# The last two products of an encoder block by one level of Strassen's scheme, in its form with fifteen sums

## The chip, the cores and the metric

One core of a Trainium2 chip runs the whole block. The metric is device time in microseconds, and lower is better. TensorE multiplies, VectorE (DVE) and ScalarE (ACT) do the work on single elements, GpSimd (POOL) adds in SBUF, and SyncE (SP) issues most of the transfers.

## The reference

512 tokens of width 2048 pass through two branches (gated DeltaNet attention and a convolution module), which are mixed with two gates. The part that matters here is what follows:

```python
gate_a, gate_b = jnp.split(jax.nn.sigmoid(gate_logits + b_gate[i]), N_BRANCHES, axis=-1)
mixed = (gate_a * y_a + gate_b * y_b) @ w_out[i]
x = x + rmsnorm(mixed, g_post[i])

e = p[i] @ w_ple_proj[i]
x = x + rmsnorm(jax.nn.sigmoid(x @ w_ple_gate[i]) * e, g_ple[i])
```

`w_out` and `w_ple_gate` are 2048 x 2048, in float32. The second product needs the normalised result of the first, and so all of its columns.

## The kernel before

Every float32 operand is split into two parts in TensorE's faster float32 format: `hi` is a cast on ACT, `lo` the rest, subtracted on VectorE. A product is then three matmuls, hi by hi, hi by lo and lo by hi, of 128 x 128 by 128 x 512 each.

Most products run in `gemm_cm` (L163), with weights as the stationary operand: a bank named `g` collects 128 output columns for all 512 tokens. `w_br_b`, the branch's last product, is interleaved with the gates of `gate_b`. The evacuation `evac_yb` (L815) forms the mixed input, 16 tiles of 128 channels by 512 tokens (`mixed`, in the profile `gt`), and the generator `split_mixed` (L826) splits them into `mh` and `ml`. It is driven by `tick`, once in some matmuls.

Then follow the two products at issue, in `gemm_tm` (L864). Here the activations are the stationary operand: a bank named `f` holds 128 tokens by 512 output columns, and four banks, one per token tile, are summed over 16 steps of 128 channels. One step uses one half of a loaded `raw` tile, split 512 wide in `prep` (L113), up to three halves ahead. w_out runs in column blocks of 512; the last block runs for the low token tiles (0, 1) and then for the high ones (2, 3), so that its weights are loaded and split twice. `out_evac` (L904) forms squares for the norm and multiplies by `g_post`. The generator `post` (L921) adds the residual and transposes x1 on TensorE (`x1t`) and splits it, low tokens beside the products of the high ones. w_ple_gate follows in the same way. Its last block is split ahead and kept whole (`hold`), and runs token tile by token tile, each with its norm and its output. The power -0.5 for a norm is a small GpSimd instruction (L889).

Each engine works through its own list in order. The lists are written by a scheduler from the program's order and the free buffers of each pool, and semaphores hold an instruction back until what it needs is there.

Of the kernel before, what the change touches and what calls it, by code (L numbers as in the profile page):

```python
# [81 lines left out]
def _body(ctx, tc, A, out):  # L82
# [30 lines left out]
    def prep():  # L113
        if not prep_src:
            return
        src = prep_src.popleft()
        raw = ring.tile([P, 1024], F32, tag="raw", name="raw", bufs=3)
        nc.sync.dma_start(raw, src)
        for q in range(2):
            rq = raw[:, q * T:(q + 1) * T]  # L120
            hi = ring.tile([P, T], F32R, tag="hi", name="hi")
            nc.scalar.copy(hi, rq)  # L122
            lo = ring.tile([P, T], F32R, tag="lo", name="lo")
            nc.vector.tensor_tensor(lo, rq, hi.bitcast(F32), ALU.subtract)  # L124
            prepped.append((hi, lo))
# [689 lines left out]
    def evac_yb(i):  # L815
        def f(ps):
            gt = gate_b[i]
            nc.vector.tensor_tensor(gt, ps, gt, ALU.mult)  # L818
            m = mixed[i]
            nc.vector.tensor_tensor(m, m, gt, ALU.add)  # L820
            added[0] += 1
        return f

    added = [0]

    def split_mixed():  # L826
        for i in range(NK):
            while added[0] <= i:
                yield
            mh = hpool.tile([P, T], F32R, tag="h", name="mh")  # L830
            nc.scalar.copy(mh, mixed[i])
            ml = hpool.tile([P, T], F32R, tag="h", name="ml")
            nc.vector.tensor_tensor(ml, mixed[i], mh.bitcast(F32), ALU.subtract)
            mixT[i] = (mh, ml)
            yield

    gemm_cm(w_in_tile(GATE_TILE0 + 16), hT, evac_gate(gate_b, 0, 16))
    gemm_cm(w_in_tile(GATE_TILE0 + 17), hT, evac_gate(gate_b, 1, 17))
    jobs.append(finish)
    for i in range(NK):  # L840
        if i + 2 < NK:
            gemm_cm(w_in_tile(GATE_TILE0 + 18 + i), hT, evac_gate(gate_b, i + 2, 18 + i))
        else:
            jobs.append(lambda i=i: spawn(split_mixed(), 6, "mix") if i == NK - 2 else None)
# [10 lines left out]
    s3 = ctx.enter_context(tc.tile_pool(name="s3", bufs=40))  # L855
# [3 lines left out]
    LOW, HIGH, ALL = (0, 1), (2, 3), (0, 1, 2, 3)  # L859

    def queue_w(w, j):
        prep_src.extend(w[j, kp] for kp in range(8))

    def gemm_tm(lhs, evac, tts=ALL, side=None):  # L864
        ps = {tt: fps.tile([P, T], F32, tag="f", name="f") for tt in tts}
        for k in range(NK):
            wh, wl = next_piece()
            if side:
                side(k)
            for tt in tts:  # L870
                lh, ll = lhs(k, tt)
                mm(ps[tt], lh, wh, start=k == 0, stop=False)  # L872
# [24 lines left out]
    def mix_lhs(k, tt):
        return [t[:, tt * P:(tt + 1) * P] for t in mixT[k]]

    def x1_lhs(k, tt):  # L900
        b = (k % 2) * 256 + (tt % 2) * P
        return [t[:, b:b + P] for t in x1T[k // 2, tt // 2]]

    def out_evac(j, gp):  # L904
        def f(tt, ps):
            junk = slots.tile([P, T], F32, tag="s", name="fjunk")
            nc.scalar.activation(junk, ps, AF.Square, accum_out=ssm[:, tt, j:j + 1])
            mg = slots.tile([P, T], F32, tag="s", name="mg")
            nc.vector.tensor_tensor(mg, ps, gp, ALU.mult)
            x1[tt][j] = mg  # L910
        return f

    def load_x_again(tts):
        xr = {}
        for j in range(4):
            for tt in tts:
                xr[tt, j] = s3.tile([P, T], F32, tag="s3", name="xr")
# [3 lines left out]
    def post(tts, xr):  # L921
        rm = inv_rms(ssm[:, tts[0]:tts[0] + 2, :], f"m{tts[0]}")
        for j in range(4):
            for n, tt in enumerate(tts):
                nc.vector.scalar_tensor_tensor(x1[tt][j], x1[tt][j], rm[:, n:n + 1], xr[tt, j], ALU.mult, ALU.add)
            yield
            for k2 in (2 * j, 2 * j + 1):
                ps = fps.tile([P, T], F32, tag="f", name="x1t")
                for n in range(4):
                    k = 2 * k2 + n // 2  # L930
                    nc.tensor.transpose(ps[:, n * P:(n + 1) * P], x1[tts[n % 2]][j][:, (k % 4) * P:(k % 4 + 1) * P], ident)
# [3 lines left out]
                nc.vector.tensor_tensor(xl, ps, xh.bitcast(F32), ALU.subtract)
                x1T[k2, tts[0] // 2] = (xh, xl)
                yield

    def stepper(gen):
        def f(k):  # L940
            next(gen, None)
        return f

    for j in (0, 1, 2, 3, 3):
        queue_w(A["w_out"], j)
    for j in (0, 0, 1, 2):
        queue_w(A["w_ple_gate"], j)
# [8 lines left out]
    for _ in pgen:
        pass

    e_t = [[None] * 4 for _ in range(NTT)]

    def load_e(j):
        for tt in range(NTT):
            e_t[tt][j] = hpool.tile([P, T], F32, tag="h", name="e")
            nc.sync.dma_start(e_t[tt][j], pe_dram[j, tt])

    held = []
    hold_raw = {}

    def hold(k):
        if k % 2 == 0:  # L970
            hold_raw[0] = ring.tile([P, 1024], F32, tag="raw", name="raw", bufs=3)
            nc.sync.dma_start(hold_raw[0], A["w_ple_gate"][3, k // 2])
        rq = hold_raw[0][:, (k % 2) * T:(k % 2 + 1) * T]
        pool, th, tl_ = (hpool, "h", "h") if k < 8 else (s3, "s3", "s3") if k < 12 else (ring, "hi", "lo")
        hi = pool.tile([P, T], F32R, tag=th, name="hi")
        nc.scalar.copy(hi, rq)
        lo = pool.tile([P, T], F32R, tag=tl_, name="lo")
        nc.vector.tensor_tensor(lo, rq, hi.bitcast(F32), ALU.subtract)
        held.append((hi, lo))

    def ple_last(gp):
        def f(tt, ps):
            e = e_t[tt][3]
            sg = slots.tile([P, T], F32, tag="s", name="fsg")
            for h in range(2):
                c = slice(h * 256, h * 256 + 256)
                nc.scalar.activation(sg[:, c], ps[:, c], AF.Sigmoid)
                nc.vector.tensor_tensor(e[:, c], sg[:, c], e[:, c], ALU.mult)
                junk = slots.tile([P, T], F32, tag="s", name="fjunk")
                nc.scalar.activation(junk[:, c], e[:, c], AF.Square, accum_out=ssp[:, tt, 3 + h:4 + h])  # L990
            nc.vector.tensor_tensor(sg, e, gp, ALU.mult)
            e_t[tt][3] = sg
        return f

    def ple_evac(j, gp):
        def f(tt, ps):
            sg = slots.tile([P, T], F32, tag="s", name="fsg")
            nc.scalar.activation(sg, ps, AF.Sigmoid)
            s = e_t[tt][j]
            nc.vector.tensor_tensor(s, sg, s, ALU.mult)  # L1000
            junk = slots.tile([P, T], F32, tag="s", name="fjunk")
            nc.scalar.activation(junk, s, AF.Square, accum_out=ssp[:, tt, j:j + 1])
            nc.vector.tensor_tensor(s, s, gp, ALU.mult)
        return f

    gp = bcast_row(A["g_ple"], 0)
    load_e(0)
    pgen = post(HIGH, xr)
    gemm_tm(x1_lhs, ple_evac(0, gp), LOW, stepper(pgen))
    for _ in pgen:  # L1010
        pass
    gemm_tm(x1_lhs, ple_evac(0, gp), HIGH)
    load_e(1)
    gemm_tm(x1_lhs, ple_evac(1, bcast_row(A["g_ple"], 1)))
    load_e(2)
    load_e(3)
    gemm_tm(x1_lhs, ple_evac(2, bcast_row(A["g_ple"], 2)), ALL, lambda k: hold(k) if k < 12 else None)
    last = ple_last(bcast_row(A["g_ple"], 3))
    for k in range(12, NK):
        hold(k)  # L1020
    for tt in range(NTT):
        ps = fps.tile([P, T], F32, tag="f", name="f")
# [67 lines left out]
```

## Time and profile before

| | us |
|---|---|
| median of 3 runs | 2553.9 (2553.58 to 2555.51) |
| profiled execution | 2555.11 |
| its span | 2553.1 |
| last `g` matmul ends, evacuation starts | 2183.6 |
| first and last start of an `f` matmul | 2184.4, 2543.4 |
| TensorE busy over the span | 2521.1 (99%) |
| VectorE busy | 1597.5 (63%) |
| ScalarE busy | 1043.1 (41%) |
| GpSimd busy | 127.3 (5%) |

The span is that of one execution under the profiler, and its own time stands 2.0 us above it. A row of a timeline or of a group names the line, the engine, the operation and output<-inputs; in brackets stands the idle time before and what ended it. PE matmuls overlap, so their rate is read from the starts.

### The profile page before, as it was taken

What the parts mean: (1) busy time and instruction counts of PE and PEld (TensorE: products, weight loads), DVE (VectorE), ACT (ScalarE), POOL (GpSimd) and SP (SyncE); (2) the same over time, 40 slices, a digit from 0 to 9 for tenths busy, and PEclk for the clock granted to TensorE, in tenths of its full rate; (3) what the DMA queues carried; (4) which work ended last, traced back from release to release, by engine and by line L of the source; (5) the groups of instructions that cost most, each with busy time, mean ns of one, the idle gap of its engine ahead of it and who ended that gap; (6) DMA issues with size and microseconds to landing.
All of it is one profiled execution on the core that took longest, in us unless ns stands there. A gap on an engine that the chain in (4) does not pass through costs nothing.

```text
span 2553.1 us, 32961 instructions
## 1 busy us (share of the span) xinstructions
PE 2521.1 (99%) x12298; PEld 2051.1 (80%) x12298; DVE 1597.5 (63%) x3024; ACT 1043.1 (41%) x2083; POOL 127.3 (5%) x135
## 2 busy tenths in 40 slices
PE   8999999999999999999999999999999999999998
PEld 7878787787878777888888888888888888888886
DVE  6775767767576766886877778947423334336644
ACT  6655455455645555322222222235322223224542
POOL 0101010000101000000000000011000000000000
PEclk9999999999999999999999999999999999999999
DMA  7322222222222222323333333343323223436542
GB/s 255 128 81 69 83 79 75 79 83 87 63 91 71 75 75 83 107 95 108 101 102 103 105 98 107 97 160 99 99 92 98 94 96 100 165 103 204 181 152 70
DMA packets 82528, 268.99 MB, mean 105 GB/s; under 512 B 9152, under 2 KB 9408, under 8 KB 82368
## 3 DMA queue, kind: packets, MB, share of 16 engines
q1 hardware_dynamic: 81216, 264.79, 32.0%
q10 hardware_dynamic: 1152, 2.10, 0.3%
q8 instruction: 96, 1.57, 0.3%
q14 instruction: 64, 0.52, 0.1%
HBM read 252.17 MB, written 14.68 MB: 105 GB/s over the span
## 4 chain that ended last, share of the span: by engine, by line
PE 88%; DVE 7%; issue 2%; ACT 2%; DMA 0%; POOL 0%; SPq 0%; DVEq 0%; POOLq 0%; ACTq 0%
PE g L180 23%; PE g L178 23%; PE g L176 22%; PE f L872 4%; PE f L874 4%; PE f L873 4%; DVE prod L589 2%; DVE lo L124 2%; DVE VT L590 2%; PE psS L467 1%; PE psB L462 1%; DVE cv L404 1%; PE psA L456 1%; PE pg L557 1%; ACT VP L601 0%
## 5 line engine op out<-in xcount | busy, mean ns | idle before, releaser
L122 ACT CAST hi<-raw 128x512 fp32r<-128x512 f32 x860 | 530.9, 623 | 1164.2 <-PE g L178 945.9
L124 DVE TENSOR_TENSOR lo<-raw,hi 128x512 fp32r<-128x512 f32 x860 | 607.8, 710 | 621.5 <-ACT hi L122 600.8
L180 PE MATMUL g<-hh,lo 128*128 128x512 f32 x2320 | 917.4, 395 | 3.7 <-DVE lo L124 2.8
L176 PE MATMUL g<-hh,hi 128*128 128x512 f32 x2320 | 914.2, 394 | 4.0 <-DVE cv L404 2.5
L178 PE MATMUL g<-hl,hi 128*128 128x512 f32 x2320 | 917.0, 395 | 0.0
L180 PEld LDWEIGHTS g<-hh,lo 128*128 128x128 f32 x2320 | 436.3, 188 | 98.5 <-DVE lo L124 14.2
L176 PEld LDWEIGHTS g<-hh,hi 128*128 128x128 f32 x2320 | 436.2, 188 | 91.5 <-issue 5.5
L178 PEld LDWEIGHTS g<-hl,hi 128*128 128x128 f32 x2320 | 436.2, 188 | 86.5 <-issue 1.6
L671 DVE SCALAR_TENSOR_TENSOR uc<-sg,vec,uc 128x483 f32<-128x483 f32 (+15 forms) x480 | 351.7, 735 | 15.0 <-ACT uc L668 5.1
L404 DVE SCALAR_TENSOR_TENSOR cv<-g,vec,cv 128x511 f32<-128x511 f32 x144 | 107.6, 747 | 2.1
L872 PE MATMUL f<-hi,mh 128*128 128x512 f32 x256 | 100.3, 392 | 0.9 <-DVE gt L818 0.9
L180 PE MATMUL g<-uh,lo 128*128 128x512 f32 x256 | 100.9, 394 | 0.0
L176 PE MATMUL g<-oh,hi 128*128 128x512 f32 x256 | 100.9, 394 | 0.0
L178 PE MATMUL g<-ol,hi 128*128 128x512 f32 x256 | 100.9, 394 | 0.0
L180 PE MATMUL g<-oh,lo 128*128 128x512 f32 x256 | 100.9, 394 | 0.0
L176 PE MATMUL g<-uh,hi 128*128 128x512 f32 x256 | 100.9, 394 | 0.0
L178 PE MATMUL g<-ul,hi 128*128 128x512 f32 x256 | 100.9, 394 | 0.0
L874 PE MATMUL f<-hi,ml 128*128 128x512 f32 x256 | 99.8, 390 | 0.0
L873 PE MATMUL f<-lo,mh 128*128 128x512 f32 x256 | 99.7, 390 | 0.0
L589 DVE TENSOR_TENSOR prod<-UT,VT 128x2 f32<-128x2 f32 (+30 forms) x248 | 87.4, 352 | 7.2
L872 PE MATMUL f<-hi,xh 128*128 128x512 f32 x192 | 76.1, 396 | 0.0
L874 PE MATMUL f<-hi,xl 128*128 128x512 f32 x192 | 75.4, 393 | 0.0
(243 smaller groups left out, 2444.7 us busy)
## 6 DMA issues: line engine op xcount, KB each, us to landing
raw<-in_w_in SPq DMA_DIRECT2D x290, 512.0 KB, 3.4
raw<-in_w_out SPq DMA_DIRECT2D x40, 512.0 KB, 3.4
raw<-in_w_ple_gate SPq DMA_DIRECT2D x40, 512.0 KB, 3.7
raw<-in_w_br_a SPq DMA_DIRECT2D x32, 512.0 KB, 3.3
raw<-in_w_br_b SPq DMA_DIRECT2D x32, 512.0 KB, 3.3
x<-in_x SPq DMA_DIRECT2D x8, 512.0 KB, 9.2
pe_dram<-e_sb SPq DMA_DIRECT2D x16, 256.0 KB, 5.0
u_dram<-uc SPq DMA_DIRECT2D x16, 256.0 KB, 2.8
```

The lines of the kernel that those rows point to most:

```text
L122: nc.scalar.copy(hi, rq)
L124: nc.vector.tensor_tensor(lo, rq, hi.bitcast(F32), ALU.subtract)
L176: mm(ps, wh, rh, start=(k == 0), stop=False)
L178: mm(ps, wh, rl, start=False, stop=False)
L180: mm(ps, wl, rh, start=False, stop=(k == NK - 1))
L404: nc.vector.scalar_tensor_tensor(y[:, s:], ps[:, 0:T - s], vv(w0 + 3 - s), y[:, s:], ALU.mult, ALU.add)
L589: nc.vector.tensor_tensor(pv_, um, vm, ALU.mult)
L590: nc.vector.tensor_reduce(VT[:, j, i0:8], pv_, AX, ALU.add)
L671: nc.vector.scalar_tensor_tensor(y[:, s:], u[:, 0:T - s], vv(w0 + TAPS - 1 - s), y[:, s:], ALU.mult, ALU.add)
L872: mm(ps[tt], lh, wh, start=k == 0, stop=False)
L873: mm(ps[tt], lh, wl, start=False, stop=False)
L874: mm(ps[tt], ll, wh, start=False, stop=k == NK - 1)
```

## The change

Tokens, channels (K) and the columns of a half of the output (1024) are each cut into two. With A the activations and B the weights, seven products take the place of eight: `P1` = A11 by B11, `P2` = A12 by B21, and five of sums: `Q5`, `P6`, `P7`, `P3`, `Q4`. The names of the sums: S1 to S4 for activations (S1 = A21 - A22, S2 = S1 - A11, S3 = A11 - A21, S4 = A12 + S2), `t` (tile `tb`) for weights. A product has 48 matmuls for one half of the columns: four pieces of 256 channels (`q`), two token tiles (`t`), two steps of 128 and three parts.

```diff
+    def split_b():
+        for k2 in range(4):
+            s1 = Sf.pop(k2)
+            s3_ = s3.tile([P, T], F32, tag="s3", name="sf")
+            for n in range(2):
...
+                nc.gpsimd.tensor_tensor(s3_[:, c], mixed[kk][:, LO], mixed[kk][:, HI], ALU.subtract)
+                nc.gpsimd.tensor_tensor(s1[:, c], s1[:, c], mixed[kk][:, LO], ALU.subtract)
+            AW["S3"][k2] = sw_split(hpool, "h", s3_)
+            yield
+            AW["S2"][k2] = sw_split(hpool, "h", s1)
...
+    def load(w, jp, blk, q):
+        raw = s3.tile([P, 1024], F32, tag="rw", name="rw", bufs=5)
+        nc.sync.dma_start(raw, w[jp, blk, q])
+        return raw
+    def e_p1(w, jp, q):
+        b11 = load(w, jp, B11, q)
+        b12 = load(w, jp, B12, q)
+        t = tb[q] = s3.tile([P, 1024], F32, tag="t", name="t", bufs=4)
+        nc.gpsimd.tensor_tensor(t, b11, b12, ALU.add)
+        return [b11]
+    def e_a(w, jp, q):
+        return e_p1(w, jp, q) + [tb[q]]
+    def e_b(w, jp, q):
+        b22 = load(w, jp, B22, q)
+        nc.gpsimd.tensor_tensor(tb[q], tb[q], b22, ALU.add)
+        b12 = load(w, jp, B12, q)
+        nc.vector.tensor_tensor(b12, b12, b22, ALU.add)
+        return [tb[q], b12, b22]
...
+    def split_piece():
+        src = sources.popleft()
...
+        hi, lo = two
+        nc.scalar.copy(hi, src)
+        nc.vector.tensor_tensor(lo, src, hi.bitcast(F32), ALU.subtract)
+        pieces.append((hi, lo))
+    def next_piece_sw(ahead=4):
+        while len(pieces) < ahead and (sources or entries):
+            while len(sources) < 2 and entries:
+                sources.extend(entries.popleft()())
+            split_piece()
+        return pieces.popleft()
...
+    def run(products, opnd, side=None):
+        ps = {}
+        for q in range(4):
+            for pr in products:
+                piece = next_piece_sw()
+                if q == 0:
+                    ps[pr] = [bank() for _ in range(2)]
+                for t in range(2):
+                    mms(ps[pr][t], pr, piece, opnd, q, t)
+                if side:
+                    side()
+        return ps
...
+    for e, w, jp in ((e_a, WO, 0), (e_b, WO, 0), (e_c, WO, 0),
+                     (e_a, WO, 1), (e_63, WO, 1), (e_p2, WO, 1), (e_p7, WO, 1), (e_t, WO, 1),
+                     (e_p1, WP, 0), (e_b21, WP, 0), (e_t, WP, 0), (e_b, WP, 0), (e_q4, WP, 0),
+                     (e_a, WP, 1), (e_early_c, WP, 1), (e_t, WP, 1), (e_p7, WP, 1), (e_p3, WP, 1)):
+        stage(e, w, jp)
...
+    def end(t, ps3):
+        fin(t, 1, add(d[t], ps3, d[t]))
+        if t == 0:
+            last(2)
+            last(3)
+        last(t)
+    run_by_token("P3", x1_opnd, end)
```

An entry `e_...` loads blocks of weights, forms sums and gives the pieces to be split; the other entries are of the same kind (`e_63`, `e_p2`, `e_p7`, `e_q4`: one GpSimd sum for each q, `e_early_c` two, `e_t`, `e_b21`, `e_p3` none). Four pairs of 1024-wide buffers hold the piece in use and three ahead. The runs of a half go, for w_out: P1 and Q5, then P6, P7, P3, then P2, Q4; in the second half P1 and Q5, P6 and P3, P2, P7, Q4. For w_ple_gate: P1, P2, Q5, then P6, P7, P3, then Q4; in the second half P1 and Q5, P2 and Q4, P6, P7, P3. Banks are combined on VectorE (with the bank as one input, L1077) and by differences on GpSimd (L1081). `split_a` forms S1 and A11 during the last `g` products, `split_c` A12 and A22 during the second run, `post_low` and `post_high` take the place of `post`: the low tokens' x1 is transposed during P7 and Q4 of w_out, the high ones' during P1 and P2 of w_ple_gate, and there `post_high` also forms S1 to S4 (12 GpSimd differences and sums, 512 wide). x1 goes out to `x1_dram` and comes back for the last sum. The order of the `w_br_b` tiles becomes 0, 8, 1, 9 and so on, and `hi` and `lo` in `prep` become halves of one tile `w`. The weights are laid out in blocks by the host's copy of the arrays, with no arithmetic.

Three places show how the lists change. The first is GpSimd's at the start of w_out (`t` and `rw` are the weight sums and the loaded weights, `sf` the activations' sums). Before:

```order
L777 TENSOR_TENSOR rst_15207<-var_15205,mhalf_c_77 128x4 [waits DVE_49]
L889 TENSOR_TENSOR rmsm0_19276<-totm0_19273,mhalf_c_77 128x2 [waits DVE_49,Pool_49]
L889 TENSOR_TENSOR rmsm2_19557<-totm2_19554,mhalf_c_77 128x2 [waits DVE_49]
L889 TENSOR_TENSOR rmsp0_20769<-totp0_20766,mhalf_c_77 128x1 [waits DVE_49]
L889 TENSOR_TENSOR rmsp1_20841<-totp1_20838,mhalf_c_77 128x1 [waits DVE_49]
```

Now, from P1 and Q5 of w_out on:

```order
L873 TENSOR_TENSOR sf_17245<-gt_11333,sf_17245 128x256
L953 TENSOR_TENSOR t_17426<-rw_17422,rw_17424 128x1024 [waits DMAHW5_49,DMAHW4_49]
L953 TENSOR_TENSOR t_17436<-rw_17432,rw_17434 128x1024 [waits DMAHW7_49,DMAHW6_49]
L873 TENSOR_TENSOR sf_17276<-gt_11633,sf_17276 128x256 [waits DVE_49]
L873 TENSOR_TENSOR sf_17276<-gt_11933,sf_17276 128x256
L953 TENSOR_TENSOR t_17450<-rw_17446,rw_17448 128x1024 [waits DMAHW1_49,DMAHW0_49]
L953 TENSOR_TENSOR t_17511<-rw_17507,rw_17509 128x1024 [waits DMAHW3_49,DMAHW2_49]
```

Where GpSimd had nothing but the powers of the norms, it now has wide and narrow sums back to back.

The second is GpSimd's list around P7 and Q4 of w_out's second half, where the power for the low tokens' norm stands (before, that power followed directly on another small instruction, in the fence above):

```order
L977 TENSOR_TENSOR rw_18497<-rw_18497,rw_18499 128x1024 [waits DMAHW6_49,DMAHW7_49,Activation_49,Pool_49]
L977 TENSOR_TENSOR rw_18518<-rw_18518,rw_18520 128x1024 [waits DMAHW0_49,DMAHW1_49,DVE_49,Pool_49]
L977 TENSOR_TENSOR rw_18539<-rw_18539,rw_18541 128x1024 [waits DMAHW3_49,DMAHW2_49,Pool_49]
L953 TENSOR_TENSOR t_18736<-rw_18732,rw_18734 128x1024 [waits DMAHW5_49,DMAHW4_49,DVE_49]
L933 TENSOR_TENSOR rmsmL_18589<-totmL_18586,mhalf_c_77 128x2 [waits DVE_49]
L953 TENSOR_TENSOR t_18771<-rw_18767,rw_18769 128x1024 [waits DMAHW7_49,DMAHW6_49,DVE_49]
```

The power now stands behind sums of weights.

The third is VectorE's list at the end (`d` takes the last product's bank, `snap` and `c11` are output tiles). Before, the last token tile:

```order
L988 TENSOR_TENSOR e_20331<-fsg_20972,e_20331 128x256 [waits Activation_49] x2
L991 TENSOR_TENSOR fsg_20972<-e_20331,grow_20685 128x512 [waits DVE_49]
L886 TENSOR_REDUCE totp3_20982<-ssp_18148 128x1 [waits Activation_49]
L887 TENSOR_SCALAR totp3_20982<-totp3_20982 128x1 [waits DVE_49]
L1033 SCALAR_TENSOR_TENSOR e_19540<-e_19540,rmsp3_20985,mg_18451 128x512 [waits Pool_49]
L1033 SCALAR_TENSOR_TENSOR e_20013<-e_20013,rmsp3_20985,mg_18745 128x512
L1033 SCALAR_TENSOR_TENSOR e_20323<-e_20323,rmsp3_20985,mg_19039 128x512
L1033 SCALAR_TENSOR_TENSOR fsg_20972<-fsg_20972,rmsp3_20985,mg_19530 128x512
```

Now, around the sum with P3's last bank:

```order
L1330 SCALAR_TENSOR_TENSOR snap_19290<-snap_19290,rmsp3_20261,x1r_20082 128x512 [waits DMAHW4_49]
L1330 SCALAR_TENSOR_TENSOR snap_19976<-snap_19976,rmsp3_20261,x1r_20084 128x512 [waits DMAHW5_49]
L1330 SCALAR_TENSOR_TENSOR snap_19802<-snap_19802,rmsp3_20261,x1r_20086 128x512 [waits DMAHW6_49]
L930 TENSOR_REDUCE totp0_20271<-ssp_17421 128x1
L1077 TENSOR_TENSOR d_20092<-f_20284,d_20092 128x512 [waits PE_49]
L931 TENSOR_SCALAR totp0_20271<-totp0_20271 128x1 [waits DVE_49]
L1330 SCALAR_TENSOR_TENSOR c11_19140<-c11_19140,rmsp0_20274,x1r_20168 128x512 [waits Pool_49]
L1330 SCALAR_TENSOR_TENSOR d_19516<-d_19516,rmsp0_20274,x1r_20170 128x512
L1330 SCALAR_TENSOR_TENSOR c11_19960<-c11_19960,rmsp0_20274,x1r_20172 128x512
L1330 SCALAR_TENSOR_TENSOR d_20090<-d_20090,rmsp0_20274,x1r_20174 128x512
L1270 TENSOR_TENSOR d_20092<-d_20092,e_19980 128x512 [waits Activation_49]
```

The outputs of three token tiles, which were spread over the last products, stand at the very end, and the last bank is taken up behind two of them.

More of the change, by code (lines that the diff above doesn't have):

```diff
@@ L820, in f @@
             nc.vector.tensor_tensor(m, m, gt, ALU.add)
-            added[0] += 1
+            added.add(i)
         return f
[L824 to L828, printed above, removed]
-                yield
[L830 to L834, printed above, removed]
-            yield
@@ L897, in mix_lhs @@
[L897 to L910, printed above, removed]
-        return f
+    ssp = fsm.tile([P, NTT, 4], F32, name="ssp")
@@ L956, in _body @@
[L956 to L979, printed above, removed]
@@ L1007, in _body @@
[L1007 to L1022, printed above, removed]
-        for k in range(NK):
-            wh, wl = held[k]
-            lh, ll = x1_lhs(k, tt)
-            mm(ps, lh, wh, start=k == 0, stop=False)
-            mm(ps, lh, wl, start=False, stop=False)
-            mm(ps, ll, wh, start=False, stop=k == NK - 1)
-        last(tt, ps)
+                ps = turn(LOW, k2)
@@ new lines, in post_late, with stepper, f, drain @@
+    def post_late():
+        while late:
+            k2, f1, s2_, s4 = late.popleft()
+            XO["S2"][k2] = sw_split(slots, "s", s2_)
+            yield
+            XO["S3"][k2] = sw_split(hpool, "h", f1)
+            yield
+            XO["S4"][k2] = sw_split(s3, "s3", s4)
+            yield
+    def stepper(gen, n=1):
+        def f():
+            for _ in range(n):
+                next(gen, None)
+        return f
+    def drain(gen):
+        for _ in gen:
+            pass
+    WO, WP = A["w_out"], A["w_ple_gate"]
@@ new lines, in _body @@
+    gen = split_b()
+    ps = run(("P1", "Q5"), mix_opnd, stepper(gen))
+    drain(gen)
+    s1 = [snap(S3_, x) for x in ps["P1"]]
+    s5 = [snap(S3_, x) for x in ps["Q5"]]
+    gp = [bcast_row(A["g_post"], j) for j in (0, 1)]
+    fin = out_fin(0, gp)
+    gen = split_c()
+    ps = run(("P6", "P7", "P3"), mix_opnd, stepper(gen))
+    drain(gen)
+    u3 = middle(ps, s1, s5, fin, S3_)
+    ps = run(("P2", "Q4"), mix_opnd)
+    for t in range(2):
+        fin(t, 0, add(s1[t], ps["P2"][t], s1[t]))
@@ new lines, in _body @@
+    gen = post_high(xr)
+    ps1 = run(("P1",), x1_opnd, stepper(gen))
+    s1 = [snap(S3_, x) for x in ps1["P1"]]
+    ps = run(("P2",), x1_opnd, stepper(gen))
+    drain(gen)
+    gp = [bcast_row(A["g_ple"], j) for j in (0, 1)]
+    fin = ple_fin(0, gp)
+    load_e(0, LOW)
+    for t in range(2):
+        fin(t, 0, add(unit(S3_, "c11"), ps["P2"][t], s1[t]))
+    load_e(1, LOW + HIGH)
+    gen = post_late()
+    ps = run(("Q5",), x1_opnd, stepper(gen, 3))
+    drain(gen)
+    s5 = [snap(S3_, x) for x in ps["Q5"]]
```

381 lines of the change are left out of this document (295 added, 86 removed).

## The prediction

> **What bounds the kernel now.** I read the page's first part and its chain, then the tile f that both changed products accumulate in, then the stretch by engine, and last the places where GpSimd adds while VectorE works.
>
> ```profile
> PE 2521.1 (99%) x12298; PEld 2051.1 (80%) x12298; DVE 1597.5 (63%) x3024; ACT 1043.1 (41%) x2083; POOL 127.3 (5%) x135
> PE 88%; DVE 7%; issue 2%; ACT 2%; DMA 0%; POOL 0%; SPq 0%; DVEq 0%; POOLq 0%; ACTq 0%
> 2184.40:2363.00 178.60, 177.92 (x800) 147.07 (x801) 74.84 (x114) 63.19 (x117) 0.71 (x1) 1.00 0.50 165
> 2363.00:2543.80 180.80, 180.15 (x802) 147.26 (x800) 92.01 (x149) 70.91 (x144) 2.37 (x4) 1.00 0.42 133
> 2543.80:2553.10 9.30, 0.00 (x0) 0.00 (x0) 4.42 (x9) 1.56 (x6) 0.55 (x1) 0.62 0.33 113
> ```
>
> The last three rows are stretches (time, busy of PE, PEld, DVE, ACT, POOL, granted clock, DMA share, GB/s): w_out, w_ple_gate, and the end after the last matmul. In the first two TensorE never rests, VectorE is busy for about half, GpSimd not at all. Any matmul taken away there is worth its full time, as long as TensorE stays fed. Its price is the spacing of starts, not the 389 ns of one, because they overlap:
>
> ```profile
> L872 PE MATMUL f<-hi,mh x256: 389/389/478, 2184.4 to 2362.5; 128*128 128x512 f32 x128
> L872 PE MATMUL f<-hi,xh x192: 387/394/482, 2363.2 to 2498.8; 128*128 128x512 f32 x192
> L1026 PE MATMUL f<-hi,xh x64: 393/394/398, 2499.5 to 2542.9; 128*128 128x512 f32 x64
> L1028 PE MATMUL f<-hi,xl x64: 389/392/397, 2499.9 to 2543.4; 128*128 128x512 f32 x64
> 2344.22 0.44 PE x1t L931 x4
> ```
>
> Each of these lines stands for three (hi, lo and the operand's lo), so there are 3 x (256 + 192 + 64) = 1536 matmuls, with 64 transposes at 0.11 us (last row) between them. (2543.4 - 2184.4 - 7.0) / 1535 = 0.229 us each.
>
> **What it removes.** Seven products of 48 matmuls for each of two column halves are 672 per product of matrices, 1344 in all: 192 fewer, 192 x 0.229 = 44.0 us. The transposes stay at 64. TensorE's own need is 1344 x 0.229 + 7.0 = 315 us.
>
> **What it adds, and where that runs.** A piece (128x1024) now feeds 12 matmuls, 2.75 us. It needs an ACT cast and a VectorE subtraction of that width, 112 of each, and, for three to four pieces in seven, a GpSimd sum of that width first: 12 + 16 + 12 + 16 = 56 over the four halves, and 8 more on VectorE (L966). TensorE sees none of this if the three pieces ahead of it (8.3 us) are always ready. The question is whether VectorE and GpSimd can work side by side, and the trace has places where they do:
>
> ```profile
> 1506.07 1.29 POOL L677 TENSOR_TENSOR acc<-acc,uc 128x512 f32<-128x512 f32 x1 [42.58 <-DVE uc L671]
> 1506.26 1.65 DVE L124 TENSOR_TENSOR lo<-raw,hi 128x512 fp32r<-128x512 f32 x1 [0.36 <-ACT hi L122]
> 1712.23 8.60 POOL L763 TENSOR_TENSOR ur<-ur,mean 128x512 f32<-128x512 f32 x5 [50.08 <-DVE mean L759]
> 1712.83 1.76 DVE L124 TENSOR_TENSOR lo<-raw,hi 128x512 fp32r<-128x512 f32 x1
> 1714.51 5.17 DVE L763 TENSOR_TENSOR ur<-ur,mean 128x512 f32<-128x512 f32 x3
> 1730.26 0.50 PE L180 MATMUL g<-hh,lo 128*128 128x512 f32 x1 [1.10 <-DVE lo L124]
> L124 DVE TENSOR_TENSOR lo<-raw,hi 128x512 fp32r<-128x512 f32 x141 | 97.1, 691 | 151.1 <-ACT hi L122 149.1 <-DMA xr<-in_x 2.0
> ```
>
> The same subtraction that takes 0.69 us through the tail (last row) takes 1.65 and 1.76 us beside a GpSimd sum; the first starts at 1506.26 and ends 0.55 us after the sum has. From 1712 on both have work without a break, and they take turns: one GpSimd sum every 8.60 / 5 = 1.72 us, one VectorE instruction every 5.17 / 3 = 1.72. So a VectorE instruction with two inputs in SBUF and a GpSimd sum do not run together; their times add up. At 1730 it reached TensorE: 1.10 us of idle. In the old tail this cannot show, since GpSimd does 6 instructions there. In the new one it is the whole matter, because the 56 sums and the 112 subtractions are all of these two kinds.
>
> **Prices.**
>
> ```profile
> 2343.95 1.28 DVE L935 TENSOR_TENSOR xl<-x1t,xh 128x512 fp32r<-128x512 f32 x2
> L988 DVE TENSOR_TENSOR e<-fsg,e 128x256 f32<-128x256 f32 x8 | 3.0, 423 | 22.0 <-ACT fsg L987 22.0
> 2546.62 2.08 DVE L1033 SCALAR_TENSOR_TENSOR e<-e,rmsp,mg 128x512 f32<-128x512 f32 x3 [0.66 <-POOL rmsp L889]
> L237 ACT ACTIVATE xjunk<-x 128x1024 f32<-128x1024 f32 x8 | 8.5, 1064 | 2.1 <-DMA x<-in_x 2.1
> raw<-in_w_out SPq DMA_DIRECT2D x40, 512.0 KB, 3.4
> ```
>
> VectorE, 512 wide: two in 1.28, 0.60 apart. From 256 wide (423 ns) to 512 (691) is 0.27 us, so 1024 comes to 0.60 + 0.53 = 1.13. The three-operand form: (2.08 - 0.75) / 2 = 0.67. GpSimd, 512 wide: 1.72 - 0.60 = 1.12 in turns, 1.29 alone; I take 1.15, and 0.6 for 256. No 1024-wide sum is in the trace: at least twice 1.12 = 2.24, at most twice 1.29 = 2.58; I take 2.4, the middle. [...] The ACT cast is taken as the 1.06 us row of that width: 112 of them are 119 us of 315, beside TensorE, and cost nothing. Loads grow from 80 to 96 of 512 KB plus 8 MB for x1's way out and back, 58 MB in some 370 us or 157 GB/s, below the 165 that the old w_out stretch already moved; nothing. The scheduler keeps DMA issue on SP and the g rows' on ACT, as before.
>
> **Shared time by stretch** (instructions with two SBUF inputs; what reads PSUM on VectorE I leave out as running beside GpSimd).
> w_out, first half: 28 splits and 4 sums of 1024 on VectorE, 36.2; operand splits 12 (S2, S3, S4) and 8 (CC) and 8 products with g_post, 28 x 0.6 = 16.8; GpSimd 12 x 2.4 = 28.8, four 512-wide differences 4.6, and 18 of split_b's 24 narrow ones 10.8 (the other six stand ahead of the stretch). 97.2 us, against 77 of TensorE.
> w_out, second half: 31.6; 8 products and 8 splits of the low tokens 9.6; 8 residuals 5.4; GpSimd 38.4 + 4.6. 89.6 against 77 and 3.5 for transposes.
> w_ple_gate, first half: 36.2; 4 + 12 operand splits and 16 products 19.2; 8 residuals 5.4; GpSimd 28.8, and 16 differences (12 of them in post_high) 18.4. 108.0 against 80.5.
> w_ple_gate, second half, up to the last split: 31.6; 10 products and sums 6.0; GpSimd 38.4 + 4.6. 80.6 against 77.
> Together 375.4 us. In each stretch it is above TensorE's time, and with 8 us of pieces ahead TensorE cannot ride over it. So the pair of VectorE and GpSimd sets the pace, and TensorE will wait for pieces.
>
> **The two ends.** Start: the new raw tiles lie in memory that uh and ul hold until the last g matmul has read them, so the first load is issued only then: 3.4 us, a cast and a split, where before TensorE went on after 0.9 us. GpSimd's narrow differences fill most of that; I add 2.
>
> ```profile
> 2183.58 0.70 DVE gt L818
> 2546.03 0.55 POOL L889 TENSOR_TENSOR rmsp<-totp,mhalf_c 128x1 f32<-128x1 f32 x1 [10.48 <-DVE totp L887]
> 2548.61 0.75 DVE L1033 SCALAR_TENSOR_TENSOR fsg<-fsg,rmsp,mg 128x512 f32<-128x512 f32 x1
> ```
>
> End: VectorE now has four output tiles of work after the last product but one (P7), with the last split between them. From that split: 2 products with g_ple 1.2, the sum with P3's low half 0.6, two products 1.2, one with e 0.6, four small ones 0.7, GpSimd's power 0.65, eight outputs and a product 6.0, the last half's sum 0.8, four outputs 2.7, two products 1.2, the square's end and two small ones 0.6, the power 0.65, four outputs 2.75: 19.7. Then 2553.1 - 2549.36 = 3.7 us from the last output's end to the span's, as now (last row above). 23.4.
>
> **The sum.** 2 + 375.4 + 23.4 = 400.8 us from the end of the last g matmul. Before it is 2553.1 - 2183.6 = 369.5. So +31.3: the 44 us saved are more than given back. Profiled execution 2555.1 + 31.3 = 2586.4; it was 1.2 us above the median of the runs, which makes 2585. Bounds: a 1024-wide sum at 2.24 or 2.58 gives 9 less or 10 more; VectorE at twice the 512 spacing (1.2) 8 more; turns that fit only nine times in ten 10 to 20 more, since VectorE waits for ACT and GpSimd for loads; a part of the work that slips into TensorE's slack of the stretch before, 10 less. 2565 to 2605.
>
> **Rivals.**
> The other side: the sums do not hold up the splits, because GpSimd gets them done while VectorE waits for ACT (149 us of such waits in the tail's L124 row) or reads PSUM. Then TensorE sets the pace: 315 us, 5 of start, 8 for the four evacuations of six banks, and at the end the 7 us before the last split less TensorE's 11 plus 23.4: 347.4, or 22 less than now, 2532. Against it: waits overlap only if total time has room, and 375 us of exclusive time do not go into 315. It decides if a 1024-wide sum holds VectorE for less than 1.85 us. 0.17.
> A longer wait: the power for the mean square of the low tokens (rmsmL) stands on GpSimd behind four sums for P7 and one for w_ple_gate, and rmsmH behind three more and two differences. VectorE's residuals wait for it in order, the splits behind them too, and TensorE's transposes for the residuals. Five sums are 12 us, three and two 9.5; if both are exposed, about 20 more: 2605 and up to 2620. 0.14.
> Clock: in the row of the end the granted clock is 0.62 over 9.3 us without a matmul; if it falls to half, it did so after 2.2 us. If TensorE's lost time comes in pauses longer than that, each restart runs slow; at 1.1 us for each of 18 runs that is 20 more, 2605. [...] The rows speak against many such pauses: a missing piece is late by 1 to 3 us. 0.08.
> No change: halfway between the first two, 0.07.
>
> **The numbers.** My forecast 0.54, longer wait 0.14, clock 0.08, faster 0.17, none 0.07. The likeliest is 2585, its own range 2565 to 2605. With the faster case and the two slower ones the range is 2535 to 2620. 0.2% is 5 us, about what a measurement here can tell from none: faster 0.17, same 0.07, slower 0.76.
>
> **What would show it.** Right: the mean of L1019 on VectorE well over its 1.22 us alone (1.7 to 2.4); L953, L964, L988 on GpSimd at 2.6 to 3.5; TensorE's idle time before L1041 and L1042 some 60 us, ended by wsp from DVE and ACT; about 20 us from the last matmul to the end. Wrong: L1019 near 1.3 us and TensorE idle for under 20 us (faster), long gaps before x1t (the power's queue), a granted clock under 0.95 in the stretch (clock).

## The result, and the profile after

The changed kernel takes 2610.2 us (median of 4 runs, 2609.5 to 2610.8) against 2553.9: slower by 2.2% (ratio 1.0219, 95% interval 1.0201 to 1.0237). The forecast was 2585 and its range 2535 to 2620. The sign held, and the loss is 56 us where 31 were forecast. The forecast's own range, 2565 to 2605, was missed by 5 us; the time lies in the part that was added for the two slower rivals.

The engines' row of the page, the granted clock in 40 slices, and the chain that ended last, of the kernel after:

```profile
PE 2506.5 (96%) x12106; PEld 2030.7 (78%) x12106; DVE 1783.6 (68%) x3052; ACT 1084.5 (42%) x2081; POOL 363.3 (14%) x251
PEclk9999999999999999999999999999999998998898
DVE 2%; DMA 1%; PE 1%; POOL 1%; issue 1%; ACT 0%; DVEq 0%; SPq 0%; POOLq 0%; ACTq 0%
```

TensorE has 192 instructions fewer (12298 before). Its busy time fell by 14.6 us only, for reasons shown below. GpSimd's busy time went from 127 to 363 us. The chain of waits could be followed over 6% of the span only, so it carries nothing here; before it was 88% PE.

The tail by stretches (length, busy of PE, PEld, DVE, ACT, POOL, granted clock, DMA share, GB/s): the start, the work up to the last split, that split with P3's last bank, and the end after the last matmul:

```profile
2186.40:2195.20 8.80, 0.05 (x1) 0.05 (x1) 3.42 (x5) 2.71 (x5) 8.01 (x11) 0.63 0.79 298
2195.20:2580.80 385.60, 334.82 (x1385) 266.03 (x1385) 348.06 (x269) 180.35 (x258) 220.53 (x95) 0.93 0.51 173
2580.80:2590.40 9.60, 8.32 (x23) 6.35 (x23) 7.60 (x16) 2.28 (x7) 1.09 (x2) 0.64 0.07 27
2590.40:2607.70 17.30, 0.00 (x0) 0.00 (x0) 11.34 (x21) 1.35 (x3) 1.10 (x2) 0.63 0.68 227
```

In the second row VectorE is busy for 348 of 385.6 us; before it was busy for 167 of 359. What TensorE waited for from 2180 us on (total, times, longest), and the group of matmuls with the longest list:

```profile
PE f L1042 <- DVE wsp L1019: 26.9, 16, 4.7
PE x1t L1129 <- DVE snap L1122: 11.5, 3, 7.2
PE f L1041 <- ACT wsp L1018: 10.0, 2, 8.8
PE f L1041 <- ACT oph L834: 5.8, 1, 5.8
PE x1t L1129 <- DVE d L1122: 4.6, 3, 2.6
L1042 PE MATMUL f<-wsp,oph x416: 387/392/797, 2205.3 to 2589.8; 128*128 128x512 f32 x139
```

These and two smaller rows are 60.7 us without a matmul. The last row says where the rest of TensorE's time went: a matmul's duration reaches 797 ns against a median of 392. From 2186.4 on, 421.3 us are 315 of need, 60.7 of waits, 17.7 from the last matmul's start to the end, and 28 more, in which matmuls after a wait ran slower. One place shows a whole such case (start, length, engine, operation, idle time before):

```profile
2222.65 2.81 POOL L964 TENSOR_TENSOR t<-t,rw 128x1024 f32<-128x1024 f32 x1
2223.17 2.83 DVE L836 TENSOR_TENSOR opl<-sf,oph 128x512 fp32r<-128x512 f32 x1
2225.93 1.21 DVE L966 TENSOR_TENSOR rw<-rw 128x1024 f32<-128x1024 f32 x1
2227.06 1.21 DVE L1019 TENSOR_TENSOR wsp<-t,wsp 128x1024 fp32r<-128x1024 f32 x1
2228.20 0.68 DVE L836 TENSOR_TENSOR opl<-sf,oph 128x512 fp32r<-128x512 f32 x1
2228.32 0.79 PE L1042 MATMUL f<-wsp,oph 128*128 128x512 f32 x1 [4.70 <-DVE wsp L1019]
2231.05 0.63 PE L1042 MATMUL f<-wsp,oph 128*128 128x512 f32 x1
2234.06 0.40 PE L1042 MATMUL f<-wsp,oph 128*128 128x512 f32 x1
```

A GpSimd sum runs from 2222.65 to 2225.46. A VectorE subtraction that takes 0.68 us by itself (2228.20) starts 0.52 us after the sum and ends at 2226.00, 0.54 us after it: it stood still through nearly all of the sum. The split that TensorE needs is behind it in VectorE's list, after one of VectorE's own weight sums (L966). TensorE idles 4.70 us, and for some 4 us after that its matmuls take 0.63 us instead of 0.39.

Groups of the tail after (count, busy, mean ns, idle before):

```profile
L1019 DVE TENSOR_TENSOR wsp<-rw,wsp 128x1024 fp32r<-128x1024 f32 x68 | 119.9, 1778 | 11.9 <-ACT wsp L1018 11.8
L1019 DVE TENSOR_TENSOR wsp<-t,wsp 128x1024 fp32r<-128x1024 f32 x44 | 80.0, 1819 | 2.6 <-ACT wsp L1018 2.5
L836 DVE TENSOR_TENSOR opl<-sf,oph 128x512 fp32r<-128x512 f32 x17 | 28.7, 1709 | 11.9 <-ACT oph L834 11.8
L953 POOL TENSOR_TENSOR t<-rw 128x1024 f32<-128x1024 f32 x16 | 41.4, 2594 | 31.1 <-DMA rw<-in_w_out 12.3 <-DVE wsp L1019 9.5 <-DVE totmL L931 5.9
L988 POOL TENSOR_TENSOR t<-t,rw 128x1024 f32<-128x1024 f32 x12 | 35.9, 3004 | 27.6 <-DMA rw<-in_w_out 16.2 <-DMA rw<-in_w_ple_gate 10.1 <-DVE wsp L1019 1.2
```

The means of L1019 hide two kinds. Its shortest, median and longest, of the larger group:

```profile
L1019 DVE TENSOR_TENSOR wsp<-rw,wsp x68: 1207/1216/3467, 2195.5 to 2580.8; 128x1024 fp32r<-128x1024 f32 x68
```

More than half of the splits take 1.21 us, and some up to 3.47: not all are slowed a little, some stand still for a whole sum. GpSimd's sums take 2.6 to 3.2 us on the mean of a group.

### The profile page after: what moved, and what is told of

It is laid out like the page before. It is cut to its first block, busy times and chain, and to the rows that moved or that the text cites. A ratio compares the mean times of both kernels' runs of the same rounds, so it can differ in the third digit from the quotient of the medians.

```text
span 2607.7 us, 32652 instructions
## 1 busy us (share of the span) xinstructions
PE 2506.5 (96%) x12106; PEld 2030.7 (78%) x12106; DVE 1783.6 (68%) x3052; ACT 1084.5 (42%) x2081; POOL 363.3 (14%) x251
## 5 line engine op out<-in xcount | busy, mean ns | idle before, releaser
L180 PE MATMUL g<-hh,w 128*128 128x512 f32 x2320 | 920.6, 397 | 13.3 <-DVE w L124 13.3
L178 PE MATMUL g<-hl,w 128*128 128x512 f32 x2320 | 916.7, 395 | 0.0
L176 PE MATMUL g<-hh,w 128*128 128x512 f32 x2320 | 915.5, 395 | 0.0
L124 DVE TENSOR_TENSOR w<-raw,w 128x512 fp32r<-128x512 f32 x716 | 505.2, 708 | 443.3 <-ACT w L123 442.1
L123 ACT CAST w<-raw 128x512 fp32r<-128x512 f32 x716 | 439.5, 620 | 838.4 <-PE g L180 819.7
L180 PEld LDWEIGHTS g<-hh,w 128*128 128x128 f32 x2320 | 436.9, 188 | 106.7 <-DVE w L124 21.5
L178 PEld LDWEIGHTS g<-hl,w 128*128 128x128 f32 x2320 | 436.9, 188 | 87.3 <-issue 1.6
L176 PEld LDWEIGHTS g<-hh,w 128*128 128x128 f32 x2320 | 437.0, 188 | 83.3 <-issue 0.2
L1042 PE MATMUL f<-wsp,oph 128*128 128x512 f32 x416 | 171.7, 413 | 26.1 <-DVE wsp L1019 26.0
L1041 PE MATMUL f<-wsp,oph 128*128 128x512 f32 x416 | 170.1, 409 | 7.0 <-ACT oph L834 5.8
L1043 PE MATMUL f<-wsp,opl 128*128 128x512 f32 x416 | 169.4, 408 | 1.3 <-DVE opl L836 1.3
L1019 DVE TENSOR_TENSOR wsp<-rw,wsp 128x1024 fp32r<-128x1024 f32 x68 | 119.9, 1778 | 11.9 <-ACT wsp L1018 11.8
L1042 PEld LDWEIGHTS f<-wsp,oph 128*128 128x128 f32 x416 | 82.2, 198 | 49.8 <-DVE wsp L1019 32.7
L1041 PEld LDWEIGHTS f<-wsp,oph 128*128 128x128 f32 x416 | 82.6, 199 | 26.4 <-ACT oph L834 6.2
L180 PE MATMUL g<-uh,w 128*128 128x512 f32 x256 | 101.0, 394 | 0.0
L180 PE MATMUL g<-oh,w 128*128 128x512 f32 x256 | 101.0, 394 | 0.0
L176 PE MATMUL g<-oh,w 128*128 128x512 f32 x256 | 101.0, 394 | 0.0
```

The source lines that it names most:

```text
L176: mm(ps, wh, rh, start=(k == 0), stop=False)
L178: mm(ps, wh, rl, start=False, stop=False)
L180: mm(ps, wl, rh, start=False, stop=(k == NK - 1))
L1019: nc.vector.tensor_tensor(lo, src, hi.bitcast(F32), ALU.subtract)
L1041: mm(ps, lh, wh[:, c], start=kk == 0, stop=False)
L1042: mm(ps, lh, wl[:, c], start=False, stop=False)
```

## The experiments

The theory: GpSimd's sums hold up VectorE's instructions with two inputs in SBUF, whatever they compute. The first rival: the sums are a longer way to each piece (load, load, sum, cast, split), and it is the pieces' lateness that costs. The second: TensorE's slow restarts.

### No weight sums, and weight sums that nobody reads

e1_nosum leaves out the 56 weight sums, so the products are of plain blocks; `t` is filled by a load. e2_idlesum has the data flow of e1, but GpSimd makes all 56 sums into a tile that nothing reads.

```diff
 def e_p1(w, jp, q):
     b11 = load(w, jp, B11, q)
-    b12 = load(w, jp, B12, q)
     t = tb[q] = s3.tile([P, 1024], F32, tag="t", name="t", bufs=4)
-    nc.gpsimd.tensor_tensor(t, b11, b12, ALU.add)
+    nc.sync.dma_start(t, w[jp, B12, q])
+    zsum(b11, t)                # e2 only: GpSimd, into an unused tile
```

> Leaves out all 56 GpSimd sums of weights (the tile t is loaded with B12 by a transfer instead of being summed; loads, casts, splits and matmuls stay as many; the weights multiplied are not the right ones). Theory 1, taking turns: the time that VectorE and GpSimd have to share falls from some 375 us to 240, under TensorE's 315; subtraction L1019 falls from 1.8 us to under 1.35, TensorE's idle time before the last matmul from 61 us to under 20; 2525 to 2545 us. Theory 2, the chain (load, sum, cast, subtraction, matmul is too long for three pieces ahead): the sums are out of the chain here too, so the same time; this run only sets the floor that the next is read against. Theory 3, memory and order alone (short buffers, in-order lists), nothing to do with the sums: stays above 2590.

> As the run without sums, but GpSimd makes all 56 sums of the same tiles into a scratch tile that nobody reads. The chain to the pieces is the short one, GpSimd's use of memory the full one. Theory 1, taking turns: L1019 (here a few lines lower) stays at 1.6 us or more, and the time goes back to 2585 to 2612 us. Theory 2, the chain: within 10 us of the run without sums, 2525 to 2550.

Measured: e1 2549.2 us (0.9982, interval 0.9973 to 0.9992), e2 2610.1 (1.0221, 1.0205 to 1.0236). The splits in the tail, of e1 and then of e2, by the two groups of pieces, with e2's largest group of sums:

```profile
L1012 DVE TENSOR_TENSOR wsp<-rw,wsp 128x1024 fp32r<-128x1024 f32 x68 | 85.7, 1262 | 45.6 <-ACT wsp L1011 41.8 <-DMA xr<-in_x 2.2 <-DMA x1r<-x_dram 1.5
L1012 DVE TENSOR_TENSOR wsp<-t,wsp 128x1024 fp32r<-128x1024 f32 x44 | 58.4, 1327 | 20.0 <-ACT wsp L1011 19.3 <-PE f L1036 0.7
```

```profile
L1023 DVE TENSOR_TENSOR wsp<-rw,wsp 128x1024 fp32r<-128x1024 f32 x68 | 125.1, 1856 | 15.3 <-ACT wsp L1022 15.3
L1023 DVE TENSOR_TENSOR wsp<-t,wsp 128x1024 fp32r<-128x1024 f32 x44 | 74.6, 1695 | 5.5 <-ACT wsp L1022 5.5
L951 POOL TENSOR_TENSOR cst<-t,rw 128x1024 f32<-128x1024 f32 x32 | 90.9, 2841 | 71.5 <-DMA rw<-in_w_out 37.1 <-DMA rw<-in_w_ple_gate 33.2
```

Sums that no split waits for cost 60.8 us, 1.09 each, and give the time of the changed kernel. The lateness of pieces through their sums adds nothing to that, and the first rival falls. The 112 splits alone take 55.6 us longer in e2 (199.7 us against 144.1). Two things more differ from e1: a buffer comes free only when its sum has read it too, and GpSimd's narrow sums and powers stand behind the idle sums in its list. TensorE's waits before x1t are 5.7 us in e1 and 19.9 in e2; how much of that comes by way of GpSimd's list is not shown.

The band of 2525 to 2545 for e1 was missed: it gains 4.6 us only. TensorE's idle time is 19.1 us, under the 20 that were expected. But from the start of the last matmul to the end it is 19.3 us, where it was 9.7 before, and TensorE is busy for 322.9 us of the tail, 8 more than its need. e5 to e9 take up what is left.

### The sums on VectorE: all, half, none

e3_dvesum puts the 56 weight sums on VectorE; e8_half does it for w_out's 28 alone.

```diff
-    nc.gpsimd.tensor_tensor(t, b11, b12, ALU.add)
+    nc.vector.tensor_tensor(t, b11, b12, ALU.add)       # e3, all seven lines of this kind
+    (nc.vector if w is WO else nc.gpsimd).tensor_tensor(t, b11, b12, ALU.add)   # e8
```

> All 56 sums of weights on VectorE, nothing left out. Theory 1, taking turns: each sum then costs 1.13 us of the shared time and not 2.4 to 2.6, so 71 us less in all, 304 us, and with its reads of PSUM VectorE has 333 us of work against TensorE's 315: 2540 to 2565 us, faster than the changed kernel by 45 to 70. A rival, that VectorE needs GpSimd's help because it is the fuller engine (370 us busy of 422 in the last part): 2610 or more.

> The changed kernel with the weight sums of w_out on VectorE and those of w_ple_gate (28 of 56) on GpSimd. If each sum on GpSimd costs its share (47 us for 56, 0.84 us each), half of it stays: 2580 to 2594. If only the crowded stretch of w_ple_gate's first half matters: 2600 or more; if only the start and w_out do: 2565 to 2575.

Measured: e3 2563.5 us (1.0038, 1.0024 to 1.0052), e8 2587.3 (1.0130, 1.0114 to 1.0145). Splits and sums of e3's tail:

```profile
L1019 DVE TENSOR_TENSOR wsp<-rw,wsp 128x1024 fp32r<-128x1024 f32 x68 | 84.8, 1249 | 8.5 <-ACT wsp L1018 8.4
L953 DVE TENSOR_TENSOR t<-rw 128x1024 f32<-128x1024 f32 x16 | 20.0, 1248 | 3.2 <-DMA rw<-in_w_out 3.2
```

With 56, 28 and none of the sums on GpSimd the times are 2610.2, 2587.3 and 2563.5: 22.9 and 23.8 us for 28 sums each, 0.83 us a sum. VectorE does such a sum in 1.25 us, less than half of GpSimd's 2.6 to 3.2 in the kernel after. The split, 1.78 us on the mean with all sums on GpSimd, is back at 1.25.

### TensorE kept warm

e4_warm adds 90 matmuls whose result is not read, in banks of their own, at four places where TensorE waits.

```diff
+    def warm(n, src):
+        ps = bank()
+        for _ in range(n):
+            mm(ps, src[:, 0:P], src, start=True, stop=True)
...
+    warm(36, AW["A11"][0][0])      # ahead of w_out; 18 before its P6, 24 and 12 in w_ple_gate
```

> The changed kernel with 90 matmuls into a bank that nobody reads, put where TensorE waits longest (36 at the start of w_out, 18 before P6 of its first half, 24 before P6 and 12 before P2 of w_ple_gate), so that it is not idle there and its clock is not lowered. Theory A, the slow restarts (28 us of the matmuls' time in the changed kernel) lie on the path: 10 to 25 us faster, 2585 to 2600. Theory B, VectorE and GpSimd set the pace and a slow restart is only taken from the next wait: within 6 us of 2610.

Measured: 2612.5 us (1.0229, 1.0214 to 1.0244), no faster than the changed kernel. The stretch 2220 to 2240, in which the case above lies, stands for the restarts in the kernel after, at a granted clock of 0.83:

```profile
2220.00:2240.00 20.00, 15.20 (x56) 11.70 (x56) 17.41 (x14) 10.84 (x17) 11.06 (x6) 0.83 0.18 59
```

In e4 the granted clock over 2186 to 2300 is 0.92, where it was 0.88. Over the tail TensorE is busy for 357.6 us, of which 20.6 are the 90 added ones (at 0.229 us), so its own 1344 matmuls and the transposes take 337 at most, against 343 after. At least 6 of the 28 us of slow time went, and the end did not come earlier. The start shows why: in e4 the first matmuls run 0.23 us apart, in the kernel after 0.43, and yet the first one with `oph` starts at 2202.32 in e4 and at 2201.97 after: in e4 it waits 1.87 us for its piece. Slow restarts are real, but these delayed an engine that had to wait for the next piece anyway. For the slow time that e4 left in place, up to 22 us, this is argued and not shown.

### Nothing but powers on GpSimd

e5_alldve moves the activation sums and the differences of banks to VectorE too (`split_a`, `split_b`, L1081, S4). e6_alldve_se also puts the first two loads into buffers that are free earlier and swaps P3 and P7 at the end; e7_dvesum_se has these two edits on e3.

```diff
-        nc.gpsimd.tensor_tensor(dst, a, b, ALU.subtract)       # L1081, and L849 to L873, L1171
+        nc.vector.tensor_tensor(dst, a, b, ALU.subtract)
...
-        raw = s3.tile([P, 1024], F32, tag="rw", name="rw", bufs=5)
+        loads[0] += 1                                          # e6, e7
+        if loads[0] <= 2:
+            raw = ring.tile([P, 1024], F32, tag="raw", name="rw", bufs=3)
+        else:
+            raw = s3.tile([P, 1024], F32, tag="rw", name="rw", bufs=5)
...
-                     ... (e_t, WP, 1), (e_p7, WP, 1), (e_p3, WP, 1)):
+                     ... (e_t, WP, 1), (e_p3, WP, 1), (e_p7, WP, 1)):
```

> All weight sums and all sums and differences of activations on VectorE too; GpSimd keeps only the powers. Taking turns: the 28 sums of 512 and 24 of 256 cost 0.6 and 0.35 us of the shared time on VectorE and not 1.15 and 0.6, some 22 us less, so VectorE has about 312 us of work, TensorE 315: 8 to 20 us faster than the run with only the weight sums on VectorE, 2543 to 2556. Rival, VectorE is now full and every move to it costs: the same or slower, 2563 to 2575.

> As e5, with two more edits: the first two loads of w_out go into the raw tiles of the ring, which do not wait for the last g matmul, and P3 comes before P7 in the last half, so that the outputs of the low tokens lie beside P7's matmuls. If the two ends cost what their rows show (8.8 us of idle at the start, 17.4 us after the last matmul against 9.3), 4 to 6 us at the start and 4 to 5 at the end: 8 to 11 faster than e5, 2534 to 2548, below the kernel before. Rival, VectorE is the bound throughout, and what is taken from the ends is waited for in the middle: within 4 of e5.

> The two edits of e6, with the sums of activations left on GpSimd (weight sums on VectorE): taking turns, 8 to 20 slower than e6; rival, faster than e6 since GpSimd takes work from a full VectorE.

Measured: e5 2555.3 us (1.0002, 0.9993 to 1.0011), e6 2556.1 (1.0004, 0.9996 to 1.0013), e7 2564.6 (1.0040, 1.0027 to 1.0052). So 8 us more come from the rest of GpSimd's sums, and the two edits give nothing. The first f matmul of e6 starts 0.88 us after the last g matmul, where the kernel after waited 8.80:

```profile
2187.53 0.47 PE L1047 MATMUL f<-wsp,ah 128*128 128x512 f32 x1 [0.88 <-DVE gt L818]
```

Some 3 us earlier than in e5 (2190.8), and yet the end is where it was. A stretch of e6 and one of e5 show where VectorE has no time left:

```profile
2187.50:2222.00 34.50, 30.80 (x129) 23.66 (x130) 34.50 (x49) 22.32 (x30) 0.00 (x0) 1.00 0.56 199
2380.00:2420.00 40.00, 33.07 (x142) 25.78 (x141) 40.00 (x53) 22.62 (x36) 0.00 (x0) 0.96 0.39 123
```

In e6's first 34.5 us VectorE is busy throughout, and the time won at the start is waited for there: a matmul that starts at 2238.59 in e5 starts at 2238.11 in e6, so 0.5 of the 3.3 us are left. e5 has a second such stretch from 2380 to 2420, where `post_high` makes the activations' sums and VectorE is busy 40.00 of 40 us. e6's last f matmul starts 1.5 us before e5's (2530.6 and 2532.1), but its end is longer (21.5 and 20.3 us), and the time is the same.

### The end shortened

e9_best changes e6 in the last half of w_ple_gate: P1 and Q5, P6, P7, Q4, P2, P3 is now the order, with the loads and buffers of that half moved to match, so that the high tokens' outputs can lie beside P2 and P3.

```diff
-                     (e_a, WP, 1), (e_early_c, WP, 1), (e_t, WP, 1), (e_p3, WP, 1), (e_p7, WP, 1)):
+                     (e_a, WP, 1), (e_6, WP, 1), (e_p7, WP, 1), (e_q4, WP, 1), (e_b21, WP, 1), (e_p3, WP, 1)):
```

> All weight and activation sums on VectorE as in e6_alldve_se, and the last half of w_ple_gate in another order of products (P1 and Q5, P6, P7, Q4, P2, P3; its loads by four fewer blocks in the last steps), so that the low tokens' sums are finished earlier and the high tokens' outputs lie beside P2 and P3. Theory (what is left over before is the end: about 21 us from the last matmul to the last output): the end falls to 10 to 13 us and the time to 2543 to 2550, below the kernel before. Rival (VectorE is full in these stretches, so work that is moved earlier is waited for there): TensorE's last matmul comes later by what the end gains, 2553 to 2558.

Measured: 2554.2 us against 2554.8 (0.9996, 0.9987 to 1.0005), no difference from the kernel before. Its tail in four stretches (about w_out's and w_ple_gate's halves) and the end:

```profile
2188.20:2276.50 88.30, 83.46 (x349) 65.91 (x350) 87.17 (x110) 50.75 (x73) 0.00 (x0) 0.98 0.51 167
2276.50:2360.00 83.50, 81.87 (x375) 66.69 (x374) 73.71 (x84) 42.48 (x59) 1.54 (x1) 1.00 0.68 228
2360.00:2445.00 85.00, 75.37 (x330) 59.43 (x329) 82.77 (x106) 47.31 (x68) 1.60 (x1) 0.98 0.54 182
2445.00:2531.30 86.30, 83.99 (x360) 68.28 (x358) 74.84 (x85) 43.17 (x66) 0.73 (x1) 0.98 0.70 247
2531.30:2552.30 21.00, 0.03 (x1) 0.00 (x0) 14.46 (x26) 1.54 (x5) 2.31 (x4) 0.56 0.58 200
```

In the first and third stretch VectorE has less than 3 us of slack, in the second and fourth 10 and 11. The end stays at 21 us. The high tokens' outputs start at 2531.61, after the last matmul, though the program writes them ahead of P3. VectorE is not what they wait for. What stands before them:

```profile
2511.58 1.29 DVE L1281 TENSOR_TENSOR u<-u,e 128x512 f32<-128x512 f32 x2
2525.84 0.69 DVE L1088 TENSOR_TENSOR d<-f,d 128x512 f32<-128x512 f32 x1 [2.01 <-PE f L1054]
2526.57 0.63 ACT L1280 ACTIVATE d<-d 128x512 f32<-128x512 f32 x1 [4.14 <-DVE d L1088]
2527.10 0.61 ACT L1283 ACTIVATE fjunk<-snap 128x512 f32<-128x512 f32 x1
2531.61 1.41 DVE L1328 SCALAR_TENSOR_TENSOR snap<-snap,rmsp,x1r 128x512 f32<-128x512 f32 x2 [0.45 <-POOL rmsp L933]
```

The last of the high tokens' products with `e` is done at 2512.9. Their squares for the norm (L1283, from 2527.10) stand in ACT's list behind the sigmoid of P3's first bank (L1280), which waits for P3's matmuls, and the norm's power and the outputs wait for the squares. So the time fell into the rival's band, 2553 to 2558, but not in the rival's way: the last matmul starts at 2530.9, as in e6 (2530.6), and the end gained nothing. ACT's list with these squares first was not tried. The three versions with everything on VectorE end within 2 us of each other.

## Why the prediction was right, and what was mis-sized

**The mechanism held.** In these runs a VectorE instruction with two SBUF inputs and a GpSimd sum took turns. e1 against e2 shows it with sums that feed nothing (60.8 us for 56), and e3, e8 and the changed kernel show it in equal steps (23.8 and 22.9 us for 28 sums each). The rows at 2222 agree (2.83 us for a 0.68 us subtraction). What the two engines share is not shown. VectorE's sums with a bank, which have one input in SBUF (L1077), are 0.68 us on the mean both after and in e5. After, none takes more than 0.69, though some lie wholly within a GpSimd sum (0.69 us from 2272.30, the sum from 2272.22 to 2274.63).

**The marks held.** L1019 is at 1.78 and 1.82 us (1.7 to 2.4 was written), the sums at 2.6 to 3.2 (2.6 to 3.5), TensorE's waits at 60.7 us (some 60), though 16.7 of them stand before x1t and not before L1041 and L1042.

**The size: 56 for 31.** By the terms of the sum, in us:

| | forecast | measured |
|---|---|---|
| start, last g bank to first f matmul | 2 | 8.8 |
| shared time up to the last split | 375.4 | 385.6 |
| from the last split to the end | 23.4 | 26.9 |
| ahead of the tail | 0 | 2.8 |
| median above the profiled span | 0.8 | 2.5 |

The differences are 6.8, 10.2, 3.5, 2.8 and 1.7, together 25. They say where the 25 us lie, not what each would give back if it were taken away.

The start is the term that was wrong in kind. It was put at a load, a cast and a split, mostly covered by GpSimd's narrow differences. But they are what is waited for, through ACT's list:

```profile
2186.43 5.35 POOL L865 TENSOR_TENSOR sf<-gt 128x256 f32<-128x256 f32 x7 [8.42 <-PE g L180]
2192.49 1.66 ACT L834 CAST oph<-sf 128x512 fp32r<-128x512 f32 x3 [14.93 <-POOL sf L849]
2194.06 1.04 ACT L1018 CAST wsp<-rw 128x1024 fp32r<-128x1024 f32 x1
2195.15 1.22 PE L1041 MATMUL f<-wsp,ah 128*128 128x512 f32 x2 [8.80 <-ACT wsp L1018]
```

ACT stands before the cast of `sf` until GpSimd's eighth difference is done, with the first weight cast behind it. In e5, where VectorE makes these differences, TensorE waits 5.17 us instead of 8.80, and with earlier loads (e6) 0.88. But it is not 6.8 us that could be had for the asking: e7 has 0.9 us of this wait where e3 has 8.7, and takes no less time (2564.6 and 2563.5).

The shared time was 10.2 us too low, inside the bounds given for it (19 less to 38 more, as a sum of the single bounds). The single prices account for little of it. VectorE's 1.13 us held: at 2225.93, 2227.06 and 2228.20 instructions start 1.13 and 1.14 us apart. A 256-wide difference on GpSimd was taken at 0.6 us and is 0.76 (seven in 5.35 us), 3 us for 18 of them. A wide sum is 2.34 us at the shortest, less than the 2.4 taken, and means of 2.6 and more hold its waits for VectorE's turn. So by these rows most of it is time between turns: VectorE is idle for 37.5 of the 385.6 us, some of it while x1t is waited for. The bound for turns that fit only nine times in ten was 10 to 20 us; how the 10.2 divide, the runs don't separate.

The end is 3.5 us longer than worked out from the last split. The 2.8 us ahead of the tail were not looked for. TensorE's waits for VectorE's splits before L180, the third of the g matmuls, grew:

```profile
PE g L180 <- DVE w L124: 11.7, 8, 2.8
```

That is up to 1000 us; before it was 1.7 us in nine waits. The change touches these splits (`hi` and `lo` became halves of one tile); whether that made it was not tried.

**The rivals.** *Longer wait* took place in small: the power rmsmL stood behind one weight sum, not five.

```profile
2363.08 0.15 DVE L931 TENSOR_SCALAR totmL<-totmL 128x2 f32<-128x2 f32 x1
2363.23 2.34 POOL L953 TENSOR_TENSOR t<-rw 128x1024 f32<-128x1024 f32 x1 [5.90 <-DVE totmL L931]
2365.52 0.70 POOL L933 TENSOR_TENSOR rmsmL<-totmL,mhalf_c 128x2 f32<-128x2 f32 x1
2367.07 0.69 PE L1129 MATMUL x1t<-cst,snap 128*128 128x128 f32 x2 [7.15 <-DVE snap L1122]
```

The sum costs 2.3 of TensorE's 7.15 us; the wait for the norm is the rest. *Clock* was in the trace (28 us of slower matmuls, and a granted clock of 0.93 where 0.95 had been named as the mark); the part of it that e4 took away was not in the time. At the end of the kernel before, the granted clock is 0.50 from 2547 us on. After the pause at 2224 the first 11 spacings of matmuls took 4.8 us, 0.43 each for the most part, where 11 times 0.229 is 2.5: a loss of 2.3 us, twice the 1.1 that this rival had put on a restart.

*Faster*, 2532, had TensorE setting the pace once GpSimd's sums hold up nothing. The condition was met in e5, e6 and e9 (no sums on GpSimd), and the result is 2554 to 2556. In e9 the f matmuls start over 343 us (2188.2 to 2530.9), 28 more than the need, and the end is 12 us longer than before: with 4 us of later start these 44 us are just what the 192 matmuls saved. By the counts of e9's rows, 32 of the third stretch being transposes, some 22 of the 28 us, an estimate, lie in the first and third stretch, where VectorE is full. So even without turns to take VectorE, with its 112 splits and 64 wide sums, sets the pace there; at the end it is ACT's list.

## What to carry to other kernels

Count an algorithm's saved matmuls against what each operand then needs on the other engines, stage by stage: here 44 us saved on TensorE brought 64 wide sums with them, and even with all of these on the faster engine for them, VectorE (1.22 us a sum in e5 and e9, on GpSimd 2.34 at the least), the tail had two stretches of four in which it was full. A GpSimd sum was not free work here beside a VectorE that subtracts tiles in SBUF (1.09 us of the kernel's time each, e2 against e1); a run with sums that nobody reads shows that price before anything is built around it. And where a stage starts or ends, look at what stands ahead in ACT's list, and whom that waits for: at the start it was the first cast, in e9 the squares of the last norm.

## What the runs showed of the hardware that was not expected

An addition of 128x1024 float32 costs less time on the busier engine: VectorE does it in 1.22 us on the mean where GpSimd has no sums beside it (e5), and GpSimd in 2.34 at the least, 2.6 to 3.2 on the mean of a group beside VectorE. Moving all 56 from GpSimd to VectorE, whose busy time was already the highest beside TensorE's, made the kernel 46.7 us faster.
